# Weight block sums in a small pool of their own, kept x queued later, two plain pairs at the change of x, other pacing (hybrid attention and mLSTM encoder layer, one core)

## The chip, the cores and the metric

The kernel runs on one core of a Trainium2 chip. The metric is the device time of one execution in microseconds (us). Engines that work side by side: TensorE (PE in the profile; its weight loads are PEld), VectorE (DVE), ScalarE (ACT), GpSimd (POOL) and SyncE (SP), whose queue issues nearly all transfers. Each engine takes its instructions in order; semaphores tie the engines together.

## The reference, cut to what matters

Sixteen learned meta tokens are put ahead of each of two sequences (1024 and 2048 tokens, width 1024, float32), and one encoder layer is applied:

```python
xn = _rmsnorm(h, g_pre)
proj = xn @ w_in + b_in                       # 1024 -> 6672
na_q, na_k, na_v, na_z, ml_qk, ml_v, ml_z, ml_o, ml_g, mg = split(proj)
ya = (neighbourhood_attention(na_q, na_k, na_v, rpb) * silu(na_z)) @ w_a
yb = (mlstm_branch(ml_qk, ml_v, ml_g, ml_o, conv_w, head_g) * silu(ml_z)) @ w_b
ga, gb = split(sigmoid(mg))                   # 2 x 1024 columns: the "gates"
y = (ga * ya + gb * yb) @ w_out
return h + _rmsnorm(y, g_post)                # meta tokens dropped at the end
```

Attention is two-dimensional over rows of 64 tokens, 8 heads of 64. The mLSTM runs forward and backward, 4 heads of 128, in chunks.

## The kernel before, in words

**Precision.** A float32 operand is split into a high part, rounded to fp32r, and a low part (value minus high part). A product is three matmuls: high x high, high x low, low x high (`mm3`, L182 to L187). So weights and x exist as pairs: whi and wlo, xh and xl.

**Two streams.** `dense` (L1919) is the stream of projections and of the final products; `sparse` (L1967) is the stream of mLSTM and attention, in the order of `STEPS`: mLSTM of the short sequence (s = 0), attention of the short one, mLSTM of the long one (s = 1), attention of the long one. `run` (L1982) weaves them: each step of the sparse stream yields a number, and dense steps (each with a cost of its own, 0.235 for a matmul of 512 columns, 0.12 for one of 256) are put behind it until that number is used up. The numbers are `A_NA` for attention, `A_D`, `A_A` and `A_G` for the mLSTM (L133). The attention of s = 0 starts with 27 such steps, then makes four for each of its 67 units in flight, and one. The output part of an mLSTM makes 34 steps a head for s = 0 and 58 for s = 1, four heads each. Where the dense stream needs attention rows that are not made yet, it says so, and the sparse stream goes on alone. The order on TensorE is the order of this program; the other engines and SP's queue are ordered by the compiler's scheduler, which goes by a simulated time line.

**The order of the projections** is `PLAN` (L41). An entry (s, t0, cols) is a group: 1024 tokens of sequence s from t0, with the columns of the mLSTM (m), of the attention (n), or the gates (g). It starts (0, 0, m), (0, 0, n), (1, 0, m), (1, 1024, m), (1, 1024, n), (1, 0, n), (1, 0, g), (1, 1024, g), (0, 0, g); then the final products follow by blocks of 512 tokens, ("f", s, b), the last ("f", 1, 3). A group has x in two halves of 512 tokens, `self.xs`. A job of a group is four blocks of 128 columns (fm: the result has columns on partitions) or one block of some 256 columns (tm: tokens on partitions). A block of fm takes 24 matmuls of 512 columns on a half of x. PSUM has three banks for the projections (pj). ScalarE and VectorE empty them into the staging tile st (four buffers), which SP stores to memory.

**x and its kept parts.** `build_half` (L443) makes the split x of a half. Groups of one range of x are not all neighbours in `PLAN`, so `xkeep` (L514) keeps the split x in memory: it puts 16 transfers of 256 KB for a half into a queue of its own, `xput`. `beside` (L523), called at each dense step of a group (a turn), issues one of them every fourth turn once 48 turns have passed; `xparts` (L354), which takes the buffers of the next half, issues all that are left. The opening group's first half is queued at the end of `opening` (L384), the second at the end of its `build_half`, whose own `xparts` empties the queue.

**Weights.** Four buffers of a hi/lo pair (`NBW`). A unit is read raw and split at its first use, and the pair is kept in memory (wh, wl) for later uses; `wtake` and `wdone` take and free units in order.

**Gates by seven products.** For the long sequence's gates (`sgates`, L866) a pair of column blocks and both halves of x are multiplied by a Strassen-Winograd scheme: seven block products of 12 matmuls each in place of eight. It needs sums of blocks of the weights, and of x. `wprep` (L536) makes the former once, in eight steps p: it loads a pair of raw blocks (pr, two buffers), forms the four sums (ps), and splits each into hi and lo (po, three buffers; ScalarE copy L560, VectorE subtraction L561), 8 stores of 512 KB for each p (L564). Its pool pq lies where the opening's pool xp was; it is started by `rows` (L480) once x of (0, 512) is scaled, moved forward by `beside` every second turn (`pace`), drained at the end of the group, and closed with its end. `tprep` (L576) makes the sums of x for a range at the start of its n group, in 28 steps, every second turn; the results are T tiles in memory, loaded by `tload` (L843). Where x changes ahead of a g group, `lead` (L777) names pairs that are multiplied plainly, with eight products, first on the first half of x and then on the second, while the second half and the T tiles are loaded. Before, that is one pair, in (1, 1024, g).

**mLSTM.** `ml` (L1340) opens its pools on the same side of SBUF as pq and xp. `ml_gates` (L1195) first loads the gate columns (g_t), works out the decay with ScalarE and VectorE, and multiplies it with a triangle (tri) on TensorE (L1233).

Of the kernel before, what the change touches and what calls it, by code (L numbers as in the profile page):

```python
# [9 lines left out]
F32 = mybir.dt.float32  # L10
F32R = mybir.dt.float32r
I32 = mybir.dt.int32
AF = mybir.ActivationFunctionType
ALU = mybir.AluOpType
# [3 lines left out]
P = 128  # L18
TCARGS = dict(schedule_with_timeline_sim=True)
D = 1024  # L20
KT = D // P
NM = 16
# [8 lines left out]
C_MQ, C_MK, C_MV, C_MZ, C_MO, C_GA, C_GB = 2048, 2560, 3072, 3584, 4096, 4624, 5648  # L31
# [98 lines left out]

NBW = 4
C512, C256 = 0.235, 0.12
A_NA, A_D, A_A, A_G = 1.085, 1.63, 1.82, 1.3  # L133


class K:
# [247 lines left out]
    def opening(self, xp):  # L384

        nc, wp, cp = self.nc, self.wp, self.cp
        self.gpre = cp.tile([P, KT], F32, name="gpre")
        nc.sync.dma_start(self.gpre, self.i["g_pre"])
        nc.vector.tensor_scalar(self.gpre, self.gpre, -0.125, None, op0=ALU.mult)
        xm = cp.tile([P, KT, NM], F32, name="xm")  # L390
        nc.sync.dma_start(xm, self.i["xm"].rearrange("p (k t) -> p k t", k=KT))
        xts = [self.xtload(0, 0, 0, xp, 9)]
        self.wload(1)
        xts += [self.xtload(0, 0, e, xp, 9) for e in (1, 2, 3)]
        self.wload(2)
# [12 lines left out]
        g = self.gpre.rearrange("p (k a) -> p k a", a=1).to_broadcast([P, KT, NM])  # L408
        nc.vector.tensor_tensor(xm, xm, g, op=ALU.mult)
        nc.scalar.activation(x[0][:, :, :NM], xm, AF.Copy)  # L410
        nc.vector.tensor_tensor(x[1][:, :, :NM], xm, x[0][:, :, :NM].bitcast(F32), op=ALU.subtract)
        for e in range(4):
            self.xsplit(x, xts[e], e, NM, self.gpre)
            if e == 0:
                self.wpump(1, 4)
        self.wpump(2, 2)
        self.wpump(3, 2, nc.vector.tensor_copy)
        res = []
        for _ in self.rsum(toks, res, (mt, NM)):
            pass  # L420
        self.rc = cp.tile([P, 9], F32, name="rc")
        self.rr = self.bp.tile([P, 2, 512], F32, name="rr", tag="gain", bufs=1)
        self.rm = cp.tile([P, NM], F32, name="rm")
        dt = self.bp.tile([P, HALF], F32, name="dt", tag="thT", bufs=1)
        dg, dm = self.rdiag(res[0], dt), dt[:NM, 512:]
        nc.vector.tensor_scalar(dm, self.ident[:NM, :NM], res[0][:NM, 4:5], None, op0=ALU.mult)
        nc.vector.tensor_copy(self.rc[:, 0:4], res[0][:, 0:4])
        nc.vector.tensor_copy(self.rc[:, 8:9], res[0][:, 4:5])
        self.wpump()
        self.wrp = self.bp, 2  # L430
        nc.gpsimd.memset(self.xmp[:, :, NM:2 * NM].bitcast(F32), 0.0)
        for a in range(2):
            nc.vector.tensor_copy(self.xmp[:, :, 2 * NM * a:2 * NM * a + NM], x[a][:, :, :NM].bitcast(F32))

        def rows():
            self.rrows(dg, self.rr[:, 0], "sm")
            p = self.psum("sm", [P, 512])
            nc.tensor.matmul(p[:, :NM], self.ones[:NM], dm, start=True, stop=True)
            nc.scalar.activation(self.rm, p[:, :NM], AF.Copy)
        self.rwait[0, 0] = rows  # L440
        self.xkeep(0, 0, x, NM)

    def build_half(self, s, t0, res):  # L443

# [12 lines left out]
        if s == 0:  # L457
# [12 lines left out]
            for e in range(4):  # L470
                self.xsplit(x, xts[e], e, 0, g)
                self.wflush(2)
                yield
            res.append(tuple(x))
            self.xkeep(s, t0, x)
            yield from self.rsum(self.toks, r)
            nc.vector.tensor_copy(self.rc[:, 4:8], r[0])
# [2 lines left out]
            def rows():  # L480
                self.rrows(dg, self.rr[:, 1], "sm")
                self.RD = self.dp.tile([P, D], F32, name="rrd")
                nc.sync.dma_start(self.RD[:, :], self.rr.rearrange("p a t -> p (a t)"))
                self.xp.close()
                self.side, self.pace = self.wprep(), 2
            self.rwait[s, t0] = rows
        else:
            bp = self.bp
# [34 lines left out]
    def beside(self):  # L523

        self.turn += 1
        if self.xput and self.turn % 4 == 1 and self.turn > 48:
            self.nc.sync.dma_start(*self.xput.popleft())
        if self.side and self.turn % self.pace == 0 and next(self.side, "end") == "end":
            self.side = None
# [6 lines left out]
    def wprep(self):  # L536

        nc = self.nc
        unit = {k: j for j, k in enumerate(_weight_units())}
        with self.tc.tile_pool(name="pq", bufs=1, side="right", reuse_waits="tile") as pool:  # L540
            raws = {}

            def load(p):
                if p < 8:
                    raws[p] = pool.tile([P, 2, 2, 512], F32, name="pr", bufs=2)
                    for f in range(2):
                        nc.sync.dma_start(raws[p][:, f].rearrange("p a c -> p (a c)"), self.i["wu"][unit["i", C_GA + (2 * p + f) * P, P], :, :D])

            load(0)
            load(1)  # L550
            for _ in range(4):
                yield
            for p in range(8):
                raw = raws.pop(p)
                sm = pool.tile([P, 4, 512], F32, name="ps", bufs=1)
                todo = [((p, "11"), (p, "12"), raw[:, 0]), ((p, "21"), (p, "22"), raw[:, 1]),
                        ((p, "s1"), (p, "s2"), sm[:, 0:2]), ((p, "s3"), (p, "s4"), sm[:, 2:4])]
                for n, (a, b, x) in enumerate(todo):
                    o = pool.tile([P, 2, 2, 512], F32R, name="po", bufs=3)
                    nc.scalar.activation(o[:, :, 0], x, AF.Copy)  # L560
                    nc.vector.tensor_tensor(o[:, :, 1], x, o[:, :, 0].bitcast(F32), op=ALU.subtract)  # L561
                    for q, key in enumerate((a, b)):
                        self.qd[key] = self.dp.tile([P, D], F32, name=f"q{p}{key[1]}")
                        nc.sync.dma_start(self.qd[key][:, :], o[:, q].rearrange("p a c -> p (a c)").bitcast(F32))  # L564
                    yield
                    if n == 0:
                        nc.vector.tensor_tensor(sm[:, 0], raw[:, 1, 0], raw[:, 1, 1], op=ALU.add)
                        nc.vector.tensor_tensor(sm[:, 1], sm[:, 0], raw[:, 0, 0], op=ALU.subtract)
                        yield
                    if n == 1:  # L570
                        nc.vector.tensor_tensor(sm[:, 2], raw[:, 0, 0], raw[:, 1, 0], op=ALU.subtract)
                        nc.vector.tensor_tensor(sm[:, 3], raw[:, 0, 1], sm[:, 1], op=ALU.subtract)
                        load(p + 2)
                        yield

    def tprep(self, s, t0):  # L576

# [198 lines left out]

    def lead(self, j):  # L777

        return [] if PLAN[j - 1][:2] == PLAN[j][:2] else [0]

    def requests(self):

# [152 lines left out]
    def group(self, s, t0, meta, cols, reuse, nxt):  # L935
# [3 lines left out]
        nb = None  # L939
        sw = (s, t0) in SW and cols == "n"  # L940
        if sw:
            self.side, self.pace = self.tprep(s, t0), 2
            sw = (s, t0, "g") in PLAN[:PLAN.index((s, t0, "n")) + 2]
        for j, (kind, c) in enumerate(jobs):
            if kind == "tm":
# [49 lines left out]
    def na(self, s, rts):  # L995
# [3 lines left out]
        with tc.tile_pool(name=f"na{s}{rts[0]}", bufs=1, side="right", reuse_waits="tile") as np_:  # L999
# [12 lines left out]
            for k in range(6):  # L1012
                next(prep, None)
                for _ in range(2 if k else 17 - 11 * s):
                    yield A_NA
            cur, nxt = self.head, None
            units = [(j, cb) for j in range(n) for cb in range(4)]
            ready = {}
# [1 line left out]
            for u in range(n_ + 4):  # L1020
                if u >= 4:
                    self.na_copy(ready[u - 4])
                if u < n_:
# [6 lines left out]
                    self.na_scores(np_, ready[u], rows)  # L1030
                    if j + 1 < n and cb == 0:
                        self.na_bias(rows, heads, j + 1)
                yield A_NA
                if u < n_:
                    self.na_exp(np_, ready[u])
                if 1 <= u <= n_:
# [4 lines left out]
                    next(prep, None)  # L1041
                if u == n_ + 3:
                    break
                yield A_NA
                if 2 <= u <= n_ + 1:
                    self.na_turn(np_, ready[u - 2])
                    if u < n_ and cb >= 2:
                        next(prep, None)
                yield A_NA
                if 2 <= u <= n_ + 1:  # L1050
                    self.na_low(ready[u - 2])
                if u >= 3:
                    self.na_out(ready[u - 3])
                yield A_NA

    def na_bias(self, rows, heads, j):

# [861 lines left out]
    def dense(self, ctx):  # L1919
# [15 lines left out]
        for j, (s, t0, cols) in enumerate(PLAN):  # L1935
# [18 lines left out]
                    self.gclose()  # L1954
            else:
                yield from self.group(s, t0, meta, cols, same[0], nxt)
                if self.side:
                    self.drain()
            meta = meta and same[1]
            if not self.done:  # L1960
# [6 lines left out]
    def sparse(self):  # L1967

        for kind, s, rts in STEPS:
            if kind == "ml":  # L1970
                for t0 in range(0, SEQLEN[s], 1024):
                    yield ("m", s, t0)
                yield from self.ml(s)
            else:
                self.mpool.close()
                types = _row_types(SEQLEN[s] // 64)
                for t0 in range(0, SEQLEN[s], 1024):
# [83 lines left out]
```

## Time and profile before

| | |
|---|---|
| time, median of 3 runs | 2818.96 us (2818.58 to 2820.68) |
| the profiled execution's own time | 2815.92 us |
| its span, first to last instruction | 2814.2 us |
| mean granted clock of TensorE | 0.982 |
| PE, PEld busy | 2703.1 us, 2379.4 us |
| DVE, ACT busy | 1887.8 us, 1394.3 us |
| POOL busy | 16.3 us |
| moved by DMA | 764.32 MB, mean 272 GB/s |

All times inside the kernel come from that one profiled execution, counted from its first instruction. A group of instructions is shown as line, engine, operation, result<-operands, shape and count. A matmul's recorded duration overlaps its neighbours', so the sum over groups is more than the busy time of the engine; the step from one start to the next says what a matmul costs in a row of them. "Idle before" is time in which the engine had nothing to run just before an instruction, with the instruction or transfer whose end released it. SPq is SP's queue: its time is that of issuing, with the waits for room included.

### The profile page before, as it was taken

What the parts mean: (1) busy time and instruction counts of PE and PEld (TensorE: products, weight loads), DVE (VectorE), ACT (ScalarE), POOL (GpSimd) and SP (SyncE); (2) the same over time, 40 slices, a digit from 0 to 9 for tenths busy, and PEclk for the clock granted to TensorE, in tenths of its full rate; (3) what the DMA queues carried; (4) which work ended last, traced back from release to release, by engine and by line L of the source; (5) the groups of instructions that cost most, each with busy time, mean ns of one, the idle gap of its engine ahead of it and who ended that gap; (6) DMA issues with size and microseconds to landing.
All of it is one profiled execution on the core that took longest, in us unless ns stands there. A gap on an engine that the chain in (4) does not pass through costs nothing.

```text
span 2814.2 us, 47371 instructions
## 1 busy us (share of the span) xinstructions
PE 2703.1 (96%) x16132; PEld 2379.4 (85%) x16132; DVE 1887.8 (67%) x5176; ACT 1394.3 (50%) x3305; POOL 16.3 (1%) x100
## 2 busy tenths in 40 slices
PE   9699799999999999999999997999999999999988
PEld 7599698889878988887798885888888998989978
DVE  4445478866657665467866754757468889798864
ACT  5332355653446455355546553555355655655531
POOL 0000000000000000000000000000000000000000
PEclk9899899999999999999999998999999999999989
DMA  9999666966697756479778889888669798998945
GB/s 364 397 387 365 238 211 229 365 204 199 213 352 267 228 194 214 158 246 341 269 251 283 278 284 351 289 284 296 190 195 303 242 323 271 298 323 265 322 163 212
DMA packets 397970, 764.32 MB, mean 272 GB/s; under 512 B 50240, under 2 KB 179216, under 8 KB 396192
## 3 DMA queue, kind: packets, MB, share of 16 engines
q1 hardware_dynamic: 396608, 758.61, 79.6%
q0 software_dynamic: 1120, 2.69, 0.4%
q8 instruction: 127, 2.08, 0.3%
q14 instruction: 115, 0.94, 0.1%
HBM read 516.46 MB, written 244.69 MB: 270 GB/s over the span
## 4 chain that ended last, share of the span: by engine, by line
PE 84%; DMA 10%; DVE 3%; ACT 1%; SPq 1%; issue 1%; DVEq 0%; POOL 0%; ACTq 0%; POOLq 0%
PE pj L185 12%; PE pj L187 12%; PE pj L186 12%; PE pj L707 5%; PE pj L708 5%; PE pj L709 5%; PE pj L890 3%; PE pj L892 3%; PE pj L891 3%; PE pj L1824 3%; PE pj L1826 3%; PE pj L1825 3%; PE sm L1173 3%; PE tr L1158 2%; DMA xl<-xl 1%; DMA xt<-xt 1%
## 5 line engine op out<-in xcount | busy, mean ns | idle before, releaser
L185 PE MATMUL pj<-xh,whi 128*128 128x512 f32 (+1 forms) x1360 | 535.7, 394 | 46.2 <-ACT st L627 23.1
L186 PE MATMUL pj<-xl,whi 128*128 128x512 f32 (+1 forms) x1360 | 523.0, 385 | 5.5 <-DMA xl<-xl 5.1
L187 PE MATMUL pj<-xh,wlo 128*128 128x512 f32 (+1 forms) x1360 | 521.8, 384 | 3.7 <-DMA wlo<-wl 3.4
L185 PEld LDWEIGHTS pj<-xh,whi 128*128 128x128 f32 x1360 | 258.5, 190 | 92.0 <-ACT st L627 23.5
L707 PE MATMUL pj<-whi,xh 128*128 128x256 f32 (+1 forms) x1152 | 329.0, 286 | 0.6 <-DVE stT L722 0.6
L708 PE MATMUL pj<-wlo,xh 128*128 128x256 f32 (+1 forms) x1152 | 324.9, 282 | 0.0
L709 PE MATMUL pj<-whi,xl 128*128 128x256 f32 (+1 forms) x1152 | 324.7, 282 | 0.0
L187 PEld LDWEIGHTS pj<-xh,wlo 128*128 128x128 f32 x1360 | 258.2, 190 | 58.1 <-DMA wlo<-wl 4.7
L186 PEld LDWEIGHTS pj<-xl,whi 128*128 128x128 f32 x1360 | 258.7, 190 | 47.7 <-DMA xl<-xl 5.6
L1824 PE MATMUL pj<-whi,mh 128*128 128x256 f32 x768 | 220.6, 287 | 0.7 <-DMA whi<-wh 0.7
L707 PEld LDWEIGHTS pj<-whi,xh 128*128 128x128 f32 x1152 | 216.9, 188 | 1.0 <-DVE stT L722 0.8
L708 PEld LDWEIGHTS pj<-wlo,xh 128*128 128x128 f32 x1152 | 217.0, 188 | 0.1
L709 PEld LDWEIGHTS pj<-whi,xl 128*128 128x128 f32 x1152 | 217.0, 188 | 0.0
L1826 PE MATMUL pj<-whi,mlo 128*128 128x256 f32 x768 | 216.3, 282 | 0.0
L1825 PE MATMUL pj<-wlo,mh 128*128 128x256 f32 x768 | 216.0, 281 | 0.0
L185 PE MATMUL pj<-yh,whi 128*128 128x512 f32 x384 | 155.0, 404 | 5.1 <-ACT yh L1742 5.1
L1165 DVE TENSOR_TENSOR pts<-tr,pts 96x384 fp32r<-96x384 f32 (+2 forms) x192 | 118.8, 619 | 57.2 <-ACT pts L1160 55.3
L187 PE MATMUL pj<-yh,wlo 128*128 128x512 f32 x384 | 152.3, 397 | 0.0
L186 PE MATMUL pj<-yl,whi 128*128 128x512 f32 x384 | 152.0, 396 | 0.0
L1160 ACT ACTIVATE pts<-tr 96x384 fp32r<-96x384 f32 (+2 forms) x192 | 103.5, 539 | 89.8 <-PE tr L1158 89.2
L1824 PEld LDWEIGHTS pj<-whi,mh 128*128 128x128 f32 x768 | 145.1, 189 | 1.8 <-DMA whi<-wh 0.9
L1825 PEld LDWEIGHTS pj<-wlo,mh 128*128 128x128 f32 x768 | 145.1, 189 | 0.9
(367 smaller groups left out, 6142.9 us busy)
## 6 DMA issues: line engine op xcount, KB each, us to landing
whi<-wh SPq DMA_DIRECT2D x160, 512.0 KB
wlo<-wl SPq DMA_DIRECT2D x160, 512.0 KB
wraw<-wu SPq DMA_DIRECT2D x48, 512.0 KB
wh<-whi SPq DMA_DIRECT2D x48, 512.0 KB
wl<-wlo SPq DMA_DIRECT2D x48, 512.0 KB
gt<-st SPq DMA_DIRECT2D x96, 256.0 KB
tg<-gt SPq DMA_DIRECT2D x96, 256.0 KB
whi<-q SPq DMA_DIRECT2D x43, 512.0 KB
```

The lines of the kernel that those rows point to most:

```text
L185: mm(out, ah, bh, start=start, stop=False)
L186: mm(out, ah, bl, start=False, stop=False)
L187: mm(out, al, bh, start=False, stop=stop)
L707: nc.tensor.matmul(o, xh, wh, start=k == 0, stop=False)
L708: nc.tensor.matmul(o, xh, wl, start=False, stop=False)
L709: nc.tensor.matmul(o, xl, wh, start=False, stop=k == KT - 1)
L890: mm(bank, w[:, 0, k], xh[:, k], start=fresh and k == 0, stop=False, skip_group_check=True)
L1160: nc.scalar.activation(pts[:ks, :nb, 0, :], pt[:ks, :nb], AF.Copy)
L1165: self.nc.vector.tensor_tensor(pts[:ks, :nb, 1, :], pt[:ks, :nb], pts[:ks, :nb, 0, :].bitcast(F32), op=ALU.subtract)
L1824: nc.tensor.matmul(o, mh[:, k, xs], wh, start=clear > 0 and k == 0, stop=False)
L1825: nc.tensor.matmul(o, mh[:, k, xs], wl, start=False, stop=False)
L1826: nc.tensor.matmul(o, ml[:, k, xs], wh, start=False, stop=clear < 2 and k == KT - 1)
```

## The change

- `A_NA` becomes `A_N`, 0.94 for s = 0 and 1.085 as before for s = 1; `A_A` goes from 1.82 to 1.79.
- The kept x of (0, 0) is queued at the end of `build_half` of (0, 512) and no longer in `opening`; the turn from which `beside` issues kept x is 64 in place of 48.
- `wprep` has one buffer each for pr and po; the sums are made in place in the raw tile, with the same 16 loads, 32 copies, 32 subtractions and 64 stores. It goes on every third turn, and from p = 5 every fifth. It is no longer drained at the end of its group; its pool stays open until the attention of s = 0 begins.
- `lead` gives two plain pairs in place of one.
- `tprep` goes on every third turn in place of every second.

```diff
-A_NA, A_D, A_A, A_G = 1.085, 1.63, 1.82, 1.3
+A_N, A_D, A_A, A_G = (0.94, 1.085), 1.63, 1.79, 1.3
...
         self.rwait[0, 0] = rows
-        self.xkeep(0, 0, x, NM)
...
             res.append(tuple(x))
+            self.xkeep(s, 0, self.xs[0], NM)
             self.xkeep(s, t0, x)
...
-                self.side, self.pace = self.wprep(), 2
+                self.side, self.pace = self.wprep(), 3
...
-        if self.xput and self.turn % 4 == 1 and self.turn > 48:
+        if self.xput and self.turn % 4 == 1 and self.turn > 64:
...
-        with self.tc.tile_pool(name="pq", bufs=1, side="right", reuse_waits="tile") as pool:
-            raws = {}
...
+        sub = lambda o, a, b: nc.vector.tensor_tensor(o, a, b, op=ALU.subtract)
+        self.pq = ExitStack()
+        pool = self.pq.enter_context(self.tc.tile_pool(name="pq", bufs=1, side="right", reuse_waits="tile"))
+        for p in range(8):
+            if p == 5:
+                self.pace = 5
+            raw = pool.tile([P, 2, 2, 512], F32, name="pr", bufs=1)
+            for f in range(2):
+                nc.sync.dma_start(raw[:, f].rearrange("p a c -> p (a c)"), self.i["wu"][unit["i", C_GA + (2 * p + f) * P, P], :, :D])
+            for _ in range(3):
                 yield
+            for f, ops in ((0, ("11", "12")), (1, ("21", "22")), (1, ("s3", "s1")), (0, ("s2", "s4"))):
+                if ops[0] == "s3":
+                    nc.vector.tensor_tensor(raw[:, 1, 1], raw[:, 1, 0], raw[:, 1, 1], op=ALU.add)
+                    sub(raw[:, 1, 0], raw[:, 0, 0], raw[:, 1, 0])
                     yield
+                if ops[0] == "s2":
+                    sub(raw[:, 0, 0], raw[:, 1, 1], raw[:, 0, 0])
+                    sub(raw[:, 0, 1], raw[:, 0, 1], raw[:, 0, 0])
+                    yield
+                o = pool.tile([P, 2, 2, 512], F32R, name="po", bufs=1)
+                nc.scalar.activation(o[:, :, 0], raw[:, f], AF.Copy)
+                sub(o[:, :, 1], raw[:, f], o[:, :, 0].bitcast(F32))
+                for q, op in enumerate(ops):
+                    d = self.qd[p, op] = self.dp.tile([P, D], F32, name=f"q{p}{op}")
+                    nc.sync.dma_start(d[:, :], o[:, q].rearrange("p a c -> p (a c)").bitcast(F32))
+                yield
+                yield
...
-        return [] if PLAN[j - 1][:2] == PLAN[j][:2] else [0]
+        return [] if PLAN[j - 1][:2] == PLAN[j][:2] else [0, 1]
...
         if sw:
-            self.side, self.pace = self.tprep(s, t0), 2
+            self.drain()
+            self.side, self.pace = self.tprep(s, t0), 3
...
-                if self.side:
+                if (s, t0) in SW and cols == "n":
                     self.drain()
...
             else:
+                if s == 0:
+                    self.drain()
+                    self.pq.close()
                 self.mpool.close()
```

In `na` each of the five `yield A_NA` becomes `yield A_N[s]`.

More of the change, by code (lines that the diff above doesn't have):

```diff
@@ L539, in wprep @@
         unit = {k: j for j, k in enumerate(_weight_units())}
-        with self.tc.tile_pool(name="pq", bufs=1, side="right", reuse_waits="tile") as pool:
-            raws = {}
[L543 to L551, printed above, removed]
-                yield
[L553 to L564, printed above, removed]
-                    yield
[L566 to L574, printed above, removed]
@@ L1014, in na @@
                 for _ in range(2 if k else 17 - 11 * s):
-                    yield A_NA
+                    yield A_N[s]
             cur, nxt = self.head, None
@@ L1032, in na @@
                         self.na_bias(rows, heads, j + 1)
-                yield A_NA
+                yield A_N[s]
                 if u < n_:
@@ L1043, in na @@
                     break
-                yield A_NA
+                yield A_N[s]
                 if 2 <= u <= n_ + 1:
@@ L1048, in na @@
                         next(prep, None)
-                yield A_NA
+                yield A_N[s]
                 if 2 <= u <= n_ + 1:
@@ L1053, in na @@
                     self.na_out(ready[u - 3])
-                yield A_NA
+                yield A_N[s]
     def na_bias(self, rows, heads, j):
```

## The prediction

> **What bounds the kernel now.** I read the page's totals first, then the waits of TensorE, then the busy time of chosen stretches, and last the chain of work and SP's queue around the worst of them.
>
> ```profile
> span 2814.2 us, 47371 instructions
> PE 2703.1 (96%) x16132; PEld 2379.4 (85%) x16132; DVE 1887.8 (67%) x5176; ACT 1394.3 (50%) x3305; POOL 16.3 (1%) x100
> ```
>
> TensorE is busy for 2703.1 of 2814.2 us, so about 111 us of idling is all that a reordering can win; the products themselves stay, but for one pair. The waits of TensorE, longest first (what waited, on whom; us in total, times, longest), say where much of that is:
>
> ```profile
> PE pj L185 <- ACT st L627: 23.1, 1, 23.1
> PE sm L1233 <- DVE g_lf L1227: 16.1, 1, 16.1
> PE pj L185 <- DMA xh<-xh: 15.2, 1, 15.2
> PE pj L186 <- DMA xl<-xl: 5.1, 1, 5.1
> PE pj L185 <- ACT yh L1742: 5.1, 1, 5.1
> ```
>
> These are four places: one stall of 23.1 us, one of 16.1, one of 15.2 + 5.1 = 20.3, and the tail's. The next view gives busy time by stretch (length, then PE, PEld, DVE, ACT, POOL, each with its count, TensorE's granted clock, DMA share, GB/s).
>
> ```profile
> 66.00:104.00 38.00, 14.94 (x64) 11.78 (x62) 10.78 (x25) 10.53 (x16) 0.26 (x2) 0.72 1.00 377
> 140.00:240.00 100.00, 100.00 (x835) 100.00 (x835) 51.20 (x75) 29.96 (x37) 0.00 (x0) 1.00 1.01 385
> 280.00:320.00 40.00, 23.94 (x100) 18.43 (x99) 13.12 (x35) 9.26 (x17) 0.68 (x12) 0.79 0.62 233
> 1060.00:1160.00 100.00, 100.00 (x507) 83.73 (x506) 55.02 (x144) 50.92 (x109) 0.00 (x0) 1.00 0.47 164
> 1704.00:1727.00 23.00, 2.68 (x11) 1.83 (x11) 5.72 (x28) 2.44 (x6) 0.00 (x0) 0.59 1.05 401
> 2460.00:2660.00 200.00, 200.00 (x1290) 181.22 (x1289) 170.71 (x430) 108.53 (x267) 1.02 (x2) 1.00 0.94 302
> 2693.50:2717.20 23.70, 13.42 (x62) 11.15 (x60) 13.34 (x46) 8.26 (x22) 0.00 (x0) 0.74 0.15 52
> 860.00:880.00 20.00, 17.89 (x88) 14.06 (x87) 18.86 (x39) 14.08 (x27) 0.00 (x0) 1.00 0.81 287
> ```
>
> The important pair is the first two rows. In both, the DMA engines are full (377 and 385 GB/s), but from 140 to 240 us TensorE does not idle at all. A full DMA system costs nothing here by itself; it costs where something TensorE needs stands behind other transfers. So the sum goes stall by stall, not by bytes.
>
> **Opening: kept x queued later, a smaller pool.** The chain of work (start, length, what) through the 23.1 us:
>
> ```profile
> 83.86 10.13 DMA pr<-wu
> 94.06 9.04 DMA mq<-st
> 103.13 0.70 ACT st L627
> 103.87 0.79 PE pj L185
> ```
>
> ScalarE cannot empty a PSUM bank, because the staging tile st is not free until its store to mq has landed. SP's queue (start, length, line, transfers) shows what that store stood behind:
>
> ```profile
> 27.20 7.71 SPq L356 DMA_DIRECT2D xh<-xh  x7
> 35.77 5.52 SPq L356 DMA_DIRECT2D xl<-xl  x8
> ...
> 53.95 1.44 SPq L1964 DMA_DIRECT2D nvm<-km  x2
> ...
> 78.55 5.64 SPq L547 DMA_DIRECT2D pr<-wu  x4
> ...
> 92.81 4.06 SPq L637 DMA_DIRECT2D mq<-st  x4
> ```
>
> The first two rows are the kept x of (0, 0), 14.1 us of SP's time from 27.20 to 41.29. If the change moves it behind row 92.81, the stall shrinks by up to 14 us. But row 53.95 is against that: L1964 is traced at the end of the first group, and yet stands in the queue well ahead of the outputs of the group's first job. So the scheduler gives SP whatever has its data as soon as it finds SP free, whatever the order of tracing. The kept x of (0, 0) has its data before 27 us and will fill the same gaps, still ahead of 92.81. What surely goes is two of the four pr loads (the new pool takes one pair of blocks at a time): 5.64 / 2 = 2.8 us. I take **3 us**; the ends are 0 and 3 + 14 = 17. A loss is excluded here, since no byte is added before 103 us.
>
> **Block sums in a pool of their own.** The chain through the 16.1 us:
>
> ```profile
> 296.15 1.05 ACT po L560
> 297.23 1.24 DVE po L561
> 298.86 5.02 DMA q7s<-po
> 304.80 2.36 DMA g_t<-gg
> 307.94 1.28 ACT L1221
> 310.86 1.07 PE sm L1233 x4
> ```
>
> The last store of the sums (q7s) lands at 303.88, and only then is g_t loaded for the gates of the short mLSTM. The reason is memory: the mLSTM's pools lie where the pq pool lay. After the change pq stays open beneath them, so g_t and the ScalarE and VectorE work behind it can run when the gate columns are stored. The tri product should then find its operand ready. I take the whole wait, **16 us** (ends 8, if SP is late with g_t, and 18, with the half-clock restart that follows).
>
> The price is in the pool: one pr and one po buffer for two and three. The same 32 copies and 32 subtractions of 1024 elements, 32 additions of 512, 16 loads and 64 stores remain, in place of sm now in raw itself. A po cycle is 1.05 + 1.24 + 5.02 us and the issue of its stores, near 8 us; four of them and an uncovered load make some 40 us for a pair, so eight pairs from 80 us end near 400, beside the first projections and the short mLSTM, instead of at 304. ScalarE adds about 4.2 us of work in 40, VectorE about 7.4 (the short additions counted half); both have room in rows like 1060 to 1160 (51 and 55 in 100). Every copy now waits for the stores before it, with the evictions of PSUM behind it in ScalarE's queue, and TensorE waits for these; three pj banks at 24 products each give some 11 us of cover against a 5.02 us landing. I put 3 us for what slips through, **together with** a denser first attention (below); ends 0 and 15.
>
> **Two plain pairs at the change of x.** TensorE's timeline around the 20.3 us, in (1, 1024, g):
>
> ```profile
> 1692.62 0.45 PE L185 MATMUL pj<-xh,whi 128*128 128x512 f32 x1
> 1692.92 0.39 PE L186 MATMUL pj<-xl,whi 128*128 128x512 f32 x1
> ...
> 1704.64 0.22 PE L1611 MATMUL sm<-v,sl 128*128 128x130 f32 x1
> 1720.11 0.80 PE L185 MATMUL pj<-xh,whi 128*128 128x512 f32 x1 [15.24 <-DMA xh<-xh]
> ```
>
> The plain pair's first half of x takes 48 products, from 1692.62 to 1704.9 with the mLSTM's work between, 12.3 us. Then the second half has not landed: DMA runs at 401 GB/s (row 1704 to 1727). A second pair on the first half gives another 12.3 us, so TensorE arrives at 1717.2 and waits 2.9 + 5.1 = 8.0. The pair done plainly costs 2 x 2 x 8 x 3 = 96 products where the seven-product form costs 7 x 4 x 3 = 84; the 12 more, at about 0.23 us (the step in the timeline, 0.3 at most), are 2.8. Net gain 12.3 - 2.8 = **9.5 us**. Ends: 17.5 if all 20.3 goes, and a loss of 2.8 if x comes later by as much. Four weight units are now held through the first half, all four buffers, but the next is freed 24 products into the second half, well ahead of its use.
>
> **Pacing.** TensorE's order is written by the program, so this part is sure in kind. Each step of attention or mLSTM releases a given amount of projection work. In before, the projections run out ahead of the attention: the last block needs the last attention rows. From 2693.5 to 2717.2 almost only attention runs:
>
> ```profile
> L1173 PE MATMUL sm<-pts,vt 104*128 104x256 f32 x25 | 6.7, 402 | 4.2 <-ACT prb L1141 3.5 <-DVE pts L1165 0.7
> ```
>
> 25 products at three or four a unit are about seven units, each of which would have carried 4 x 1.085 = 4.3 of projections: a shortage near 31. The change withholds 0.145 in each of the 296 steps of the first attention (27 + 4 x 67 + 1), that is 42.9, and 0.03 in the 368 output steps of both mLSTMs, 11.0; the plain pair adds 2.8 of work. 56.7 is more than 31, so the last attention ends with projections still to do, and the tail has no gap. That stretch had 23.7 - 13.42 = 10.3 us idle, and its busy part ran at a clock of 0.74: at 0.12 us a product (835 in 100 us, row 140 to 240) its 62 are only 7.4 us of work, 16 lost. I take **14 us** (ends 5 and 16). A denser first attention raises its engines by about an eighth; from 1060 to 1160 that is harmless, in a window like 860 to 880 (VectorE 18.86 of 20) it may add a few us, which the 3 above covers.
>
> The slower pace of tprep I cost at nothing (ends 4 either way): its 28 steps still finish before they are drained, in 84 turns of about 96, and TensorE meets none of it but by the T tiles.
>
> **The sum.** 3 + 16 + 9.5 + 14 - 3 = 39.5 us. Against the profiled execution's own 2815.92 this gives 2776.4; the median of the runs, 2818.96, is 3.0 above that execution, so I forecast **2779 us**.
>
> **Rivals.**
> 1. *Single buffers hold ScalarE up: slower.* In the chain of the opening a store (mq<-st) took 9.04 us, not 5.02. If the scheduler puts po copies ahead of evictions while the DMA engines are that full, each of the 32 holds ScalarE, and VectorE behind it, for up to 9 us. The cover is 11 us in the fm jobs; a tm job fills a bank with 24 products at 0.12 us (835 in 100 us, row 140 to 240), 2.9 us, so it has 5.8 with two banks ahead. It turns the change into a loss when more than (39.5 + 3) / 32 = 1.3 us of each copy is exposed; at 2 us, 64 us in place of the 3, the time is 2840. For it: the mq row. Against it: from 140 to 240 us TensorE lost nothing though such copies ran then, with more buffers. The Trainium skill ("Trainium Kernel Development and Optimization", Best Practices) advises to double-buffer so that transfers overlap compute, which this change undoes; by that rule it would be this case. The trace of before, where the copies are buffered, cannot settle it. Chance 0.13.
> 2. *The moves do not reach the chip's order.* The scheduler fills as before, g_t stays late behind busy transfers, the second half of x arrives no sooner relative to TensorE; what stays is the tail and half of 16: 14 + 8 - 2.8 - 3 = 16, 2803. Chance 0.20, of which 0.05 is for within 0.2% (another few us lost to new collisions of attention with the loads of x).
> 3. *The opening recovers too.* The kept x does go behind row 92.81: 14 more, 2765; with all of the 20.3 as well, 2757. Chance 0.17.
> 4. The forecast, 2768 to 2792: chance 0.50.
>
> **How the numbers follow.** 0.2% (5.6 us) is about what a measurement of this kernel tells from no change. Faster: 0.50 + 0.17 + 0.15 = 0.82; same 0.05; slower 0.13. For 8 in 10 the range runs from 2753 (case 3's far end, with a little from tprep) to 2812: it leaves out the slower case, most of "same", and a few in a hundred below.
>
> **What would show it.** After the change the wait of L1233 on g_lf is gone, or under 2 us; the stall at the second half of x is near 8 us; the gap on yh before the last block is gone and that block starts with attention well past. The wait on st L627 is still there near 20 us if the scheduler fills gaps as I read it, and near 6 if not. The stores of q7s land near 400 us. I am wrong if ScalarE's waits of po on q stores total tens of us with TensorE idle beside them, if g_t is still loaded just before its use, or if new stalls appear where x is changed near 750 us.

## The result, and the profile after

The changed kernel takes **2776.64 us** (median of 4 runs, 2773.44 to 2781.17) where the kernel before takes 2818.77 (4 runs beside it, 2817.52 to 2820.68): a ratio of 0.9851, 95% interval 0.9834 to 0.9868. The profiled execution took 2777.01 us, against 2815.92 before: 38.9 us less. Its totals and, in a second fence, TensorE's longest waits (what waited, on whom; us in total, times, longest; the lines of `fm_evac` are seven lower than before, so L620 is the copy that was L627):

```profile
span 2775.2 us, 47355 instructions
PE 2701.9 (97%) x16144; PEld 2378.1 (86%) x16144; DVE 1879.9 (68%) x5174; ACT 1389.2 (50%) x3302; POOL 16.9 (1%) x100
```

```profile
PE pj L185 <- ACT st L620: 22.6, 1, 22.6
PE sc L1568 <- DVE q L1522: 7.1, 1, 7.1
PE pj L185 <- DMA wlo<-q: 6.3, 2, 3.6
```

TensorE's busy time is the same to 1.2 us, and its idle time falls from 2814.2 - 2703.1 = 111.1 to 2775.2 - 2701.9 = 73.3 us. Of the five waits shown of before, the first is still there, g_lf, x and yh are gone, and two new ones have come. Seven stretches hold nearly all of the difference. Busy time by stretch (length, then PE, PEld, DVE, ACT, POOL with their counts, granted clock, DMA share, GB/s), first before, then after:

```profile
40.00:120.00 80.00, 52.93 (x209) 41.66 (x208) 30.67 (x60) 27.30 (x39) 0.36 (x3) 0.81 0.99 380
280.00:340.00 60.00, 43.57 (x186) 33.45 (x185) 24.85 (x71) 21.07 (x44) 0.68 (x12) 0.86 0.62 221
400.00:520.00 120.00, 119.28 (x780) 107.25 (x779) 98.31 (x293) 68.37 (x175) 0.61 (x5) 1.00 0.72 245
740.00:880.00 140.00, 130.72 (x594) 104.75 (x593) 98.21 (x223) 71.86 (x133) 1.17 (x4) 0.98 0.88 312
1300.00:1400.00 100.00, 89.96 (x442) 75.15 (x442) 88.86 (x263) 59.98 (x151) 0.20 (x2) 0.97 0.82 276
1660.00:1740.00 80.00, 59.68 (x286) 49.44 (x285) 38.36 (x126) 31.88 (x83) 0.10 (x1) 0.87 0.92 337
2660.00:2720.00 60.00, 49.63 (x338) 46.00 (x337) 41.37 (x119) 30.27 (x81) 0.00 (x0) 0.88 0.41 133
```

```profile
40.00:120.00 80.00, 54.72 (x220) 43.18 (x219) 26.43 (x55) 24.88 (x39) 1.20 (x15) 0.83 0.94 355
280.00:340.00 60.00, 59.65 (x332) 49.98 (x331) 36.77 (x100) 29.48 (x68) 0.43 (x3) 1.00 0.81 294
400.00:520.00 120.00, 109.29 (x630) 94.02 (x629) 98.65 (x263) 70.13 (x162) 0.61 (x5) 0.96 0.88 312
740.00:880.00 140.00, 132.17 (x627) 106.48 (x626) 103.65 (x238) 81.87 (x155) 1.94 (x8) 0.99 0.95 339
1300.00:1400.00 100.00, 96.36 (x498) 80.91 (x497) 88.51 (x259) 59.75 (x154) 0.10 (x1) 0.98 0.95 319
1660.00:1740.00 80.00, 73.40 (x351) 60.80 (x350) 47.90 (x174) 35.61 (x96) 0.00 (x0) 0.94 0.97 353
2660.00:2720.00 60.00, 60.00 (x330) 52.11 (x329) 33.43 (x64) 10.84 (x28) 0.00 (x0) 1.00 0.81 294
```

Length less PE busy is idle time, row by row: 27.1 to 25.3 in the opening, 16.4 to 0.4 at the gates of the short mLSTM, **0.7 to 10.7** between 400 and 520 us, 9.3 to 7.8, 10.0 to 3.6, 20.3 to 6.6 at the change of x, 10.4 to 0 in the tail. The sums are 94.2 and 54.4: 39.8 us less in these rows, the whole difference and 2 us that are lost again outside them (111.1 - 73.3 = 37.8). So the change wins in five places, gives 10 us back in one, and leaves the largest stall of all where it was.

### The profile page after: what moved, and what is told of

The parts are those of the page before. It is cut to its first block, busy times and chain, and to the rows that moved or that the text cites. A ratio compares the mean times of both kernels' runs of the same rounds, so it can differ in the third digit from the quotient of the medians.

```text
span 2775.2 us, 47355 instructions
## 1 busy us (share of the span) xinstructions
PE 2701.9 (97%) x16144; PEld 2378.1 (86%) x16144; DVE 1879.9 (68%) x5174; ACT 1389.2 (50%) x3302; POOL 16.9 (1%) x100
## 4 chain that ended last, share of the span: by engine, by line
PE 50%; DMA 3%; DVE 1%; ACT 1%; issue 0%; SPq 0%; DVEq 0%; ACTq 0%
PE pj L185 7%; PE pj L187 7%; PE pj L186 7%; PE pj L1818 3%; PE pj L1820 3%; PE pj L1819 3%; PE pj L883 3%; PE pj L885 3%; PE pj L884 3%; PE sm L1167 2%; PE tr L1152 2%; PE pj L700 1%; PE pj L701 1%; PE pj L702 1%; DMA t2h<-t2h 1%; PE sm L187 0%
## 5 line engine op out<-in xcount | busy, mean ns | idle before, releaser
L185 PE MATMUL pj<-xh,whi 128*128 128x512 f32 (+1 forms) x1376 | 541.9, 394 | 30.7 <-ACT st L620 22.6
L187 PE MATMUL pj<-xh,wlo 128*128 128x512 f32 (+1 forms) x1376 | 528.1, 384 | 1.2 <-DMA wlo<-wl 0.9
L185 PEld LDWEIGHTS pj<-xh,whi 128*128 128x128 f32 x1376 | 261.4, 190 | 76.0 <-ACT st L620 23.1
L1159 DVE TENSOR_TENSOR pts<-tr,pts 96x384 fp32r<-96x384 f32 (+2 forms) x192 | 118.9, 619 | 71.0 <-ACT pts L1154 69.5
```

What stands on the lines that cost most here:

```text
L185: mm(out, ah, bh, start=start, stop=False)
L187: mm(out, al, bh, start=False, stop=stop)
L1159: self.nc.vector.tensor_tensor(pts[:ks, :nb, 1, :], pt[:ks, :nb], pts[:ks, :nb, 0, :].bitcast(F32), op=ALU.subtract)
```

## The experiments

Three theories were to be told apart. *Opening:* the stall of 22.6 us is made by the kept x, which the scheduler pulls into SP's gaps whatever is traced when (against: it is made by the loads and weights of the opening). *Between 400 and 520 us:* the new idle time comes from the single buffers of the block sums (against: from the work of the engines there). *The other gains:* each belongs to the part of the change that the prediction gave it to (against: things moved, and other places came out better by themselves). Each time is a median of four or five runs, given with the ratio to the kernel before, measured beside it, and its 95% interval. The kernel before came out between 2815.5 and 2818.8 us in these rounds, so a difference of two medians and the same difference by ratios can lie up to 4 us apart; where it matters both are given. The idle times that the expectations name (24 and 12, 16.8 and 6.4, 18, 14 us) are larger than those of the tables above (20.3 and 6.6, 10.0 and 3.6, 16.4, 10.7); the tables decide.

### One plain pair

```
-        return [] if PLAN[j - 1][:2] == PLAN[j][:2] else [0, 1]
+        return [] if PLAN[j - 1][:2] == PLAN[j][:2] else [0]
```

> The changed kernel with one plain pair at the change of x instead of two. Theory (the second pair buys the loader of x its time, worth about 9.5 us net): near 2786 us, and about 24 us of idle TensorE between 1680 and 1720 us, most of it waiting for x, instead of about 12. Rival (the wait was only passed from x to the second pair's weights): within 3 us of 2776.6, with the same idle time in that stretch under another name.

Measured: 2788.51 us, 0.9898 (0.9883 to 0.9914), 11.9 us above the changed kernel (13 by the ratios). Its longest wait in the stretch, and the stretch:

```profile
PE pj L185 <- DMA xh<-xh: 19.3, 1, 19.3
```

```profile
1660.00:1740.00 80.00, 60.30 (x299) 50.33 (x298) 44.34 (x160) 34.12 (x91) 0.10 (x1) 0.87 0.96 348
```

The wait for x is back at 19.3 us and the idle time at 19.7. The theory holds: the second pair is worth about 12 us, near the 9.5 of the forecast. The rival, that the wait only changed its name, holds for a third of it: with two pairs 6.3 us of waiting for the second pair's weights (wlo from q) is left.

### The T parts at the old pace

```
-            self.side, self.pace = self.tprep(s, t0), 3
+            self.side, self.pace = self.tprep(s, t0), 2
```

> The changed kernel with the generator of the T parts called at every 2nd step as before instead of every 3rd. Theory A (the slower calls took away the idle time between 1300 and 1400 us, which went from 16.8 to about 6.4 us and which the forecast had priced at nothing): near 2787 us, with some 17 us idle there again. Theory B (that stretch lies better because the steps ahead of it moved): within 3 us of 2776.6, idle time there still near 6.

Measured: 2775.64 us, 0.9848 (0.9833 to 0.9862).

```profile
1300.00:1400.00 100.00, 97.07 (x504) 81.97 (x503) 89.29 (x265) 60.39 (x156) 0.10 (x1) 0.98 0.98 328
```

2.9 us idle, as with the new pace: theory B. The pace of `tprep` does nothing that these runs can tell, and the 6.4 us won there belong to something else.

### The old pacing

```
-A_N, A_D, A_A, A_G = (0.94, 1.085), 1.63, 1.79, 1.3
+A_N, A_D, A_A, A_G = (1.085, 1.085), 1.63, 1.82, 1.3
```

> The changed kernel with the costs per step of the two attentions as before (1.085 for both, 1.82). Theory (the pacing alone empties the tail's wait, 14 us by the forecast, 5 to 16): near 2790 us, with the wait of TensorE on yh between 2680 and 2720 us back at about 17 us. Rival (the tail is better because everything ahead of it ends earlier): within 4 us of 2776.6, with no such wait.

Measured: 2786.73 us, 0.9898 (0.9881 to 0.9915): undoing the pacing costs 10.1 us (13 by the ratios). Waits and stretches:

```profile
PE tr L1699 <- DVE hb L1694: 13.7, 1, 13.7
...
PE pj L185 <- ACT yh L1736: 3.6, 1, 3.6
```

```profile
2660.00:2720.00 60.00, 52.94 (x248) 43.12 (x248) 37.18 (x92) 15.21 (x40) 0.00 (x0) 0.91 0.61 218
1300.00:1400.00 100.00, 86.30 (x479) 74.56 (x478) 83.66 (x262) 54.67 (x141) 0.20 (x2) 0.93 0.83 280
```

The wait on yh is back, with 7.1 us idle in the tail, not the 17 that was expected. And 13.7 us are idle between 1300 and 1400: the stretch that `tprep`'s pace did not touch answers to the pacing. The two add up to more than 10.1 us (7.1 + 13.7 - 3.6 = 17.2 us of idle time against the changed kernel), so some of it is paid for in small pieces elsewhere, about 7 us by the medians, 4 by the ratios: 8.2 us are idle between 400 and 520 with the old pacing, not 10.7, and 3.8 between 1660 and 1740, not 6.6. The run puts both numbers back together, A_N and A_A, so their shares stay open.

### The block sums as before

`wprep` of the kernel before (pr in two buffers, po in three, sums in ps, pace 2, its pool closed by the generator) in the changed kernel, and the two `drain`s as before:

```
+        with self.tc.tile_pool(name="pq", bufs=1, side="right", reuse_waits="tile") as pool:
...
-                if s == 0:
-                    self.drain()
-                    self.pq.close()
```

> The changed kernel with the block sums made as before: double buffers, sums in a tile of their own, every 2nd step, the pool closed by the generator. Two terms of the change go back together here: the wait of the gates (about 18 us between 280 and 340 us) returns, and the idle time that is new between 420 and 500 us (about 14 us) goes. Theory (the single buffers cost about 14 us where the forecast had 3): near 2781 us. Rival (they cost the 3 us of the forecast, the new idle time has another cause): near 2792 us, with the idle time between 420 and 500 us still there.

Measured: 2781.76 us, 0.9883 (0.9868 to 0.9897): 5.1 us above the changed kernel (9 by the ratios), as the theory said.

```profile
PE sm L1234 <- DVE g_lf L1228: 16.2, 1, 16.2
```

```profile
400.00:520.00 120.00, 120.00 (x785) 108.06 (x784) 100.33 (x304) 70.36 (x180) 0.60 (x5) 1.00 0.73 246
```

The gates wait 16.2 us again, and nothing is idle between 400 and 520. So the smaller pool buys 16 us and costs 7 to 11 of them. The run puts back the buffers, the pace and the closing of the pool at once; it does not part them.

### Two half tiles in the same bytes

```
-                o = pool.tile([P, 2, 2, 512], F32R, name="po", bufs=1)
-                nc.scalar.activation(o[:, :, 0], raw[:, f], AF.Copy)
...
+                for q, op in enumerate(ops):
+                    o = pool.tile([P, 2, 512], F32R, name="po", bufs=2)
+                    nc.scalar.activation(o[:, 0], raw[:, f, q], AF.Copy)
+                    sub(o[:, 1], raw[:, f, q], o[:, 0].bitcast(F32))
```

> The changed kernel with the output tile of the block sums cut in two: two tiles po of one operand each in the same bytes, so that one can be filled while the other is stored; twice as many, half as wide instructions on ScalarE and for the low parts on VectorE. Theory (the single tile, through ScalarE's waits for its store, makes the idle time between 420 and 500 us): 6 to 12 us faster than the changed kernel, 2765 to 2771 us, and waits of ScalarE for the stores of po near zero. Rival (VectorE, 19 of 20 us busy at 460 to 480 us, is the bound there): 2774 to 2782 us, the idle time as large as it was though the waits on po go.

Measured: 2769.74 us, 0.9834 (0.9821 to 0.9847), 6.9 us below the changed kernel. The instructions on po, changed kernel first (operation, how many; ns min/median/max, first and last start in us), and who waited for what (us, times), then the same of the half tiles:

```profile
L561 ACT ACTIVATE po<-pr x32: 1040/1059/1069, 88.9 to 507.1; 128x1024 fp32r<-128x1024 f32 x32
...
L565 SPq DMA_DIRECT2D q0s<-po x4: 418/603/1183, 118.9 to 130.2; - x4
...
L565 SPq DMA_DIRECT2D q4s<-po x4: 320/452/497, 299.2 to 321.6; - x4
...
L565 SPq DMA_DIRECT2D q7s<-po x4: 320/428/697, 497.3 to 515.0; - x4
...
  DMA q<-po: 15.2, 7
  DMA pr<-wu: 9.3, 3
```

```profile
L562 ACT ACTIVATE po<-pr x64: 611/628/635, 89.1 to 426.3; 128x512 fp32r<-128x512 f32 x64
...
  DMA q<-po: 16.3, 10
  DMA pr<-wu: 15.1, 5
```

```profile
400.00:520.00 120.00, 117.54 (x694) 101.85 (x693) 104.83 (x304) 73.78 (x180) 0.61 (x5) 1.00 0.88 303
```

The time came out as the theory said, and its reason did not. ScalarE waits no less for stores and loads; what changed is that the last copy of the sums starts at 426 us instead of 507, and the idle time between 400 and 520 falls from 10.7 to 2.5. In the changed kernel the sums still run when x of (1, 0) is built and the short mLSTM is under way. ScalarE's timeline ahead of the new wait of 7.1 us, which ends with q at 487 us:

```profile
468.40 1.06 ACT L561 ACTIVATE po<-pr 128x1024 fp32r<-128x1024 f32 x1 [3.10 <-DMA q<-po]
...
482.94 1.06 ACT L331 ACTIVATE xsq<-xr 128x1024 bf16<-128x1024 f32 x1 [2.29 <-DMA xr<-x_sample]
...
486.60 0.40 ACT L1521 ACTIVATE q<-cv 128x256 fp32r<-128x256 f32 x1
```

One copy of the sums stood 3.1 us behind its store, with evictions and the copies of x behind it, and then ScalarE waited 2.3 us for a load of x, with q behind that. So the single buffers cost little while the sums run beside the first projections (between 120 and 400 us TensorE is idle for 0.4 us in all) and much when they **end late and meet** the building of x. That the late end is the cause is argued: the half tiles change the length of each copy and the number of buffers along with it.

### The kept x tied behind

Each store of a kept x is made to issue after the last SP instruction traced before it:

```
-            self.nc.sync.dma_start(*self.xput.popleft())
+            with ExitStack() as st:
+                for y in reversed(self.nc.cur_bb.bb.instructions):
+                    if y.engine == mybir.EngineType.SP:
+                        st.enter_context(self.tc.issue_after(y))
+                        break
+                self.nc.sync.dma_start(*self.xput.popleft())
```

> The changed kernel with each store of a kept x tied behind the last instruction traced on SyncE's queue, so that the scheduler can't pull it into gaps ahead of the first mq stores. Theory (the 23 us of SyncE time of the kept x ahead of the store at 92.44 us is what holds the buffer st, and so the wait of TensorE on ScalarE, 22.6 us, in the opening): that wait falls below 6 us and the time to about 2758 us (2755 to 2765). Rival 1 (the wait is made by the loads and weights of the opening, not by the kept x): the wait stays above 18 us and the time within 3 us of 2776.6. Rival 2 (it goes, but the kept x then stands in the way of the block sums' stores between 150 and 300 us): the wait goes and the time stays within 6 us of 2776.6.

Measured: **2747.16 us**, 0.9749 (0.9735 to 0.9764), faster than both kernels, and more than the theory asked. SP's queue (start, length, line, transfers), of the changed kernel and then of this one (L527 has become L537, L630 is L640):

```profile
42.84 3.72 SPq L527 DMA_DIRECT2D xh<-xh  x4
...
59.84 3.16 SPq L527 DMA_DIRECT2D xh<-xh  x6
...
92.44 3.17 SPq L630 DMA_DIRECT2D mq<-st  x4
```

```profile
39.62 0.50 SPq L537 DMA_DIRECT2D xh<-xh  x1
...
65.61 2.73 SPq L640 DMA_DIRECT2D mq<-st  x2
```

```profile
PE sc L1578 <- DVE q L1532: 6.0, 1, 6.0
...
PE pj L185 <- ACT st L630: 2.3, 1, 2.3
```

```profile
40.00:120.00 80.00, 77.66 (x393) 65.13 (x392) 36.97 (x70) 33.57 (x51) 1.20 (x15) 1.00 0.98 372
400.00:520.00 120.00, 111.87 (x564) 92.75 (x563) 104.60 (x310) 78.34 (x180) 0.60 (x5) 0.97 0.94 331
740.00:880.00 140.00, 136.23 (x759) 116.65 (x758) 110.56 (x245) 86.03 (x172) 0.00 (x0) 1.00 0.95 329
```

In the changed kernel all kept x of (0, 0) and (0, 512), 32 stores of 256 KB, went out between 36 and 75 us, ahead of the mq stores at 92.44; at 355 GB/s, the stretch's rate, their 8.4 MB are 23.6 us of transfer, the size of the stall. With the tie two of them go early, the first mq stores of that row go at 65.61, and the wait falls from 22.6 to 2.3 us. The DMA system is as full as before (372 GB/s). It was the order, not the amount. The gain is above 22.6 us: all idle time falls by 24.1 us (73.3 to 2743.5 - 2694.3 = 49.2), 23.0 of it in the first row (25.3 to 2.3), and TensorE's busy time falls by 7.6 (2701.9 to 2694.3) for the same 16144 products, with the granted clock of the opening at 1.00 in place of 0.83. The first attention has 4 us less idle (7.8 to 3.8).

### Which half of it the change had done

The same tie in the kernel before (in it the kept x of (0, 0) is queued in the opening):

> The kernel before with the same tie of the kept x behind SyncE's traced order. Theory (the wait in the opening is the kept x's in both kernels, whatever the rest of the change): the wait of about 23 us goes and the time falls by 23 to 30 us to 2787 to 2795 us. Rival (in the kernel before the block sums' double loads, 1 MB each, take the same place in the queue): less than 8 us, 2809 or more.

Measured: 2803.25 us, 0.9949 (0.9935 to 0.9962), 14 us only; neither expectation. Then the tie in the changed kernel with the early queuing put back, and the early queuing put back alone:

```
+        self.xkeep(0, 0, x, NM)
...
-            self.xkeep(s, 0, self.xs[0], NM)
```

> The kept x tied behind SyncE's traced order, but queued in the opening as before the change, from where it is emptied at once when the next x is built. Theory (the change's later queuing does nothing alone, but is what a tie needs, because the stores of the first x are otherwise traced ahead of the last mq store): the wait in the opening back at about 15 us, 2760 to 2765 us. Rival (the other kernel's smaller gain came from its block sums): the wait near 2 us, 2745 to 2750 us.

> The changed kernel with the first kept x queued in the opening as before, no tie: one part of the change undone. Theory of the prediction (the scheduler fills SyncE's gaps in either case, 3 us at most): 2774 to 2780 us, the wait in the opening at 22 to 24 us. Rival (the later queuing brings something by itself): 2783 us or more.

Measured: 2769.31 us, 0.9834 (0.9817 to 0.985) with the tie, above both of its ranges; 2773.24 us, 0.9852 (0.9838 to 0.9865) without, a little below its own. The wait in the opening of the three, kernel before with the tie, changed kernel queued early with the tie, and without:

```profile
PE pj L185 <- ACT st L637: 17.0, 2, 14.6
```

```profile
PE pj L185 <- ACT st L630: 12.2, 1, 12.2
```

```profile
PE pj L185 <- ACT st L620: 21.2, 1, 21.2
```

Queued early, the sixteen stores of (0, 0) are traced before the last mq store of the first job, so the tie leaves them ahead of it, and half of the stall or more stays (12.2 of 22.6 us, and 14.6 of 23.1 in the kernel before). Queued later without a tie nothing changes (3 us by the medians, inside the spread of the runs, and none by the ratios). The change's "kept x queued later" is half of a remedy: with the tie it is worth 22 us (2769.31 - 2747.16), alone nothing that these runs can tell. The other half of that change, kept x from turn 64 in place of 48, was not undone by itself.

### Two attempts to go further

Loads of the T parts traced after the first half of the plain pairs, with the kept x tied:

```
-                    self.tload(s, t0, (1, 2, 3))
...
+            if hf == 1 and self.tlate:
+                self.tload(s, t0, (1, 2, 3))
```

> The kernel with the kept x tied behind, and the loads of the three T parts at the change of x traced after the plain pairs' first half instead of ahead of them. Theory (the second pair's weights come late because they stand behind 12 loads of 256 KB): the wait for wlo from q (5.9 us) and most of the 10.7 us idle between 1660 and 1700 us go, 2738 to 2742 us. Rival (the loads then come late for their first use and the wait only changes its name): 2745 to 2750 us.

Measured: 2748.06 us, 0.9757 (0.9744 to 0.9771): nothing. Tracing them later did not move them: the first T load goes out at 1642.80 us, against 1644.75 in the kernel above, between the same weights. So the next two kernels have both remedies, tie and half tiles, and the second of them ties the T loads behind as well:

> The kept x tied behind and the output tile of the block sums cut in two, in one kernel. If the two gains are separate places they add up less what the first has already taken between 420 and 500 us (there 50.3 - 33.9 = 16 us of idle TensorE became 10): 2739 to 2743 us. If the tie has moved the collision away from the block sums: 2745 to 2749 us, nothing more.

> As the one with both, and the loads of the three T parts tied behind the plain pairs' weights and x on SyncE, which tracing them later did not do. Theory (at the change of x the DMA engines are full, and what is needed last stands ahead of what is needed first): the waits on wlo from q there go, 6 to 11 us less than the kernel with both. Rival (the bytes are the bound, not their order): within 3 us of it, with a wait for a T part in place of the one for the weights.

Measured: 2756.8 us, 0.9792 (0.9778 to 0.9806), and 2755.35 us, 0.9789 (0.9775 to 0.9804). Waits of the first, then of the second:

```profile
PE sc L1577 <- DVE nwt L161: 7.6, 1, 7.6
PE sm L1176 <- ACT prb L1144: 6.5, 4, 3.1
PE pj L185 <- DMA wlo<-q: 6.3, 2, 3.4
```

```profile
PE sm L1184 <- ACT prb L1152: 8.1, 4, 4.4
...
PE tr L1456 <- DVE kf L1420: 4.1, 2, 3.7
```

Half tiles and tie do not add up: together they are 9.6 us *slower* than the tie alone (12 by the ratios), outside both expectations. With the tie the kept x stores run beside the sums, which end at 471.74 us with half tiles (last store) and at 482.23 without, so nothing is gained between 400 and 520; and the first attention waits 6.5 us for its probabilities (prb), with the tie alone 1.8. Why its order comes out worse is not settled. Tying the T loads moved them (the first goes out at 1694.2 us, not 1660.1) and removed the wait on wlo, and no T part came late, but TensorE then waits 3.7 us at once for the mLSTM's kf in the same stretch, and the time stays within 1.5 us. The fastest kernel of the study is the changed one with the kept x tied.

## Why the prediction was right, step by step

The forecast of 2779 us and the time of 2776.64 agree, and so do the sums, 39.5 us forecast and 39.8 by the two tables of stretches. One term was far off and two were somewhat too large; places that no term had, or had too small, made up for it.

- **Opening, 3 us.** Right in mechanism and size: 1.8 us less idle, the stall on L620 22.6 us, where the forecast had about 20. The step that the scheduler fills SP's gaps with whatever has its data was tested from both sides: a later place in the trace alone changes nothing, a tie removes the stall. What the forecast missed is that the stall's bytes were those of both kept halves, not of (0, 0) alone: rival 3 priced 14 us, and the tie took 20.3 off the wait.
- **Gates, 16 us.** Right: g_t is loaded at 175.3 and 190.7 us in place of 304.3 and 304.8, the wait on g_lf is gone, and it comes back at 16.2 us with the old pool.
- **Block sums, -3 us.** This is the step that failed, in size and in its way. It put the end of the sums "near 400 us"; the last store goes out at 515. Two sizes were off. From q0s at 118.9 to q4s at 299.2 a pair takes 45 us, not 40; and the generator's own `self.pace = 5` from the sixth pair on was not counted: the last three take 66 each (q4s at 299.2 to q7s at 497.3). That the pace made this difference fits the program, but no run changes it alone. The stretch from 400 to 520 lost 10.0 us in place of 3; going back to the old sums shows 7 to 11 (16.2 at the gates less 5.1 to 9 in all). The prediction named ScalarE's waits for stores of q, tens of us with TensorE idle beside them, as a sign of being wrong. The first half of that sign came (15.2 us on the row shown), the second only between 400 and 520 us. With the half tiles these waits stay and the idle time goes once the sums end earlier, so the size of the waits does not set the cost. What the trace shows in its place is the meeting with the building of x.
- **Single buffers, the slower rival.** It had the right place and too high a price: about 0.3 us for each of the 32 copies (10.0 / 32), where 1.3 was the point from which it decides. The Trainium skill ("Trainium Kernel Development and Optimization", Best Practices) advises double-buffering; here the trace agrees in part, since two half tiles in the same bytes are 6.9 us faster, and does not where it counts: the change is 42 us faster without them, and with the tie the half tiles lost.
- **Two plain pairs, 9.5 us.** Right in size: 20.3 - 6.6 = 13.7 us of idle time less the 2.8 of products is 10.9, and undoing it costs 11.9 to 13. Wrong in what would be left: not 8.0 us of waiting for x, but none for x and 6.3 for the second pair's weights.
- **Pacing, 14 us.** 10.1 to 13 by undoing it, inside its ends. The tail is empty of idle time as forecast (10.4 to 0), but undoing the pacing brings back 7.1 of that; the rest came from elsewhere. Not foreseen: that the stretch from 1300 to 1400 hangs on the pacing too (6.4 us won there, 10.1 lost when it is undone), and that some 4 to 7 us go back in small pieces; the forecast had put a denser attention into the 3 us of the block sums.
- **T parts, 0.** Right: 2775.64 us with the old pace. And no new stall came where x is changed near 750 us (9.3 to 7.8 us idle).

So the sum holds by some luck. In idle time, 7.0 us too little cost for the block sums, 3.6 too much gain in the tail and 1.2 in the opening stood against 6.4 us at 1300, 1.5 between 740 and 880, and 4.2 at the change of x (2.8 of which are the added products, which idle time does not count). Undone one at a time, the second pair, the pacing and the sums cost 11.9 + 10.1 + 5.1 = 27.1 us together by the medians and 35 by the ratios, of the 42 that the change brings. The 7 to 15 us that are missing may be won by parts that stand in for one another, or may be the spread of the runs, since each ratio is known only to about 4 us; pairs of parts were not undone, so this stays open.

## What to carry to other kernels

Where a scheduler orders the queues, a move in the program is not a move on the chip: look in the queue's own timeline for the moved instruction before crediting it, and tie it to its neighbour if it did not move. When a producer that runs beside others is slowed or paced, forecast **where it ends and whom it meets there**, from its calls and not only from its own chain. Undo each part by itself before explaining a total that fits: here a good total held one term that was three times too small.

## What the runs showed of the hardware

A full DMA system did not by itself stall TensorE: with the tie the opening ran at 372 GB/s and TensorE was busy for 77.66 of 80 us, while at 355 GB/s and the wrong order it was busy for 54.72. Halving a ScalarE copy from 128x1024 to 128x512 took it from 1.06 to 0.63 us, so two halves cost 1.26: about 0.2 us for each extra instruction. And the stall's price is higher than its length: in the opening, the granted clock over 80 us was 0.83 with the stall and 1.00 without, and the same products took 7.6 us less busy time in all.
